# The corner blocks of a triangular inverse: a second path through DRAM replaced by products with the identity

## The chip, the cores and the metric

The kernel runs on one core of a Trainium2 chip. The metric is device time in microseconds (us) of one execution, as the median of several runs. The engines are TensorE (PE; its weight loads are PEld), VectorE (DVE), ScalarE (ACT), GpSimd (POOL) and SyncE (SP), which issues most transfers.

## The reference

Two layers of a decoder trunk on 256 tokens of width 1024: feed-forward, a mixer of three branches, attention to a memory, feed-forward. The change lies in one branch of the mixer, a recurrence with a state per head (8 heads of width 64):

```python
    def step(state, inp):
        r_t, w_t, k_t, v_t, kk_t, a_t = inp
        sa = jnp.einsum('bhij,bhj->bhi', state, kk_t)
        state = (state * w_t[:, :, None, :]
                 - sa[..., None] * (kk_t * a_t)[:, :, None, :]
                 + v_t[..., None] * k_t[:, :, None, :])
        return state, jnp.einsum('bhij,bhj->bhi', state, r_t)
```

The kernel takes it in chunks of 64 tokens, and a chunk needs the inverse of a unit lower triangular 64x64 matrix for each head.

## The kernel before

The trunk is float32. Large products split each weight into a high part (`whi`, by ACT) and a low part (`wlo`, by DVE, from the raw load and `whi`), and take three float32r products for one. Raw weights land in three buffers (`raw0` to `raw2`), the parts in eight each. A raw load on SP therefore waits until DVE has made the last `wlo` from that buffer.

The order on every engine is not written by hand. `Program` records all operations, builds their dependences and orders them with a list scheduler that has costs for each operation. It takes a transfer to last

```python
    DMA_START, DMA_END, DMA_RATE = 1.1, 0.95, 360e3
```

us around its bytes, and records the program several times over, keeping the order that it thinks shortest. So a small edit can move operations anywhere. Each engine then works its list strictly in that order: what stands behind a waiting instruction waits as well.

The tokens are taken in two halves, t = 0 and 1. For each, in each of the two layers, these steps run beside the large products of the mixer; the four solves are called A (layer 0, t=0), B (layer 0, t=1), C (layer 1, t=0) and D (layer 1, t=1).

- `rwkv_front` makes the 64x64 matrices and writes their diagonal 32x32 blocks to DRAM (`sl`), to be read back with one block in each partition (`XL`).
- `rwkv_solve` inverts the 32x32 blocks by 31 elimination steps on DVE. The result `XX` holds, in a partition for each block and group of columns, the columns of the inverse. ACT transposes the free axes of it into `TM` (the "transposing copy", 128x256), SP writes `TM` to DRAM (`sx`, four writes) and reads it back (four reads) into `XT`, where the transposed inverses stand as diagonal blocks. Besides, SP writes `XX` itself to DRAM (`si`, one write) and reads two quarters of it back into `X1` (two reads): the same diagonal blocks, not transposed.
- `rwkv_back` reorders `X1` into `XN` (two ACT copies, 32x256), then fills the off-diagonal corner of the inverse: the products of `LN` and `XT` (16 of 32x32, into banks `b_ya`), two copies by ACT into `HH`, the products of `XN` and `HH` (16 more), and a negated copy into `XT`. The full products with `XT` follow.

The banks of PSUM have four names with two each: `g` for the large products, `ya`, `yb` and `s` for the rest. All operations are issued from one line (L415), so the profile names them by engine and tile: `heap` is the heap that holds XX, TM, XT, X1, XN and HH alike, and `heapr` that of the float32r tiles.

Of the kernel before, what the change touches and what calls it, by code (L numbers as in the profile page):

```python
# [12 lines left out]
F32 = mybir.dt.float32  # L13
# [463 lines left out]
class Trunk:  # L477
# [730 lines left out]
    def rwkv_solve(self, l, t):  # L1208

        nc, h = self.nc, self.h  # L1210
        rt = self.rt[t]
        XL, XX, TM = rt["XL"], rt["XX"], h.alloc(256)
        XT = rt["XT"] = h.alloc(1024)
        nc.gpsimd.memset(XT.ap, 0.0)
        _, sx, si = self.scr[l][t]
        eng = getattr(nc, self.SOLVE)
        xlv = XL.v("p (i j) -> p i j", j=32)
        xx, tm = XX.v("p (i c) -> p i c", c=8), TM.v("p (i c) -> p i c", c=8)
        for j in range(31):
            n, m = 31 - j, j // 4 + 1  # L1220
            self.tt(tm[:, 0:n, 0:m], xlv[:, j + 1:32, j:j + 1].to_broadcast([128, n, m]),
                    xx[:, j:j + 1, 0:m].to_broadcast([128, n, m]), MULT, eng)
            self.tt(xx[:, j + 1:32, 0:m], xx[:, j + 1:32, 0:m], tm[:, 0:n, 0:m], SUB, eng)
        nc.sync.dma_start(si, XX.ap)
        X1 = rt["X1"] = h.alloc(256)
        for q in (0, 2):
            nc.sync.dma_start(X1[32 * q:32 * q + 32, :].rearrange("p (b c) -> p b c", c=8),
                              si.rearrange("(q b) (i c) -> q i b c", q=4, c=8)[q])
        nc.scalar.copy(TM.v("p (c i) -> p c i", c=8), XX.v("p (i c) -> p c i", c=8))
        sxw = sx.rearrange("(b a) (c x i) -> x b (a c) i", a=4, c=2, x=4)  # L1230
        for x in range(4):
            nc.sync.dma_start(sxw[x], TM.v("p (c i) -> p c i", c=8)[x:128:4])
        xt = XT.v("p (h n) -> p h n", h=8)
        sxv = sx.rearrange("(q h a) (c i) -> q (a c) h i", q=4, h=8, c=8)
        for q in range(4):
            nc.sync.dma_start(xt[32 * q:32 * q + 32, :, 32 * q:32 * q + 32], sxv[q])
        h.free(XL, XX, TM)
# [18 lines left out]
    def rwkv_back(self, l, t):  # L1256

        self.rwkv_values(t)
        nc, h = self.nc, self.h
        rt = self.rt[t]  # L1260
        XT, X1, LN, ln, PA, BA, pa, ba, MM, mmv, VS = (
            rt[k] for k in ("XT", "X1", "LN", "ln", "PA", "BA", "pa", "ba", "MM", "mmv", "VS"))
        vs = VS.v("p (c h n) -> p c h n", c=2, h=8)
        xt = XT.v("p (h n) -> p h n", h=8)
        HH = h.alloc(256)
        XN = h.alloc(256)
        for b in (0, 64):
            nc.scalar.copy(XN.v("p (h c x) -> p h c x", h=8, x=4)[b:b + 32], X1.v("p (h x c) -> p h c x", h=8, x=4)[b:b + 32])
        x1, hh = XN.v("p (h n) -> p h n", h=8), HH.v("p (h n) -> p h n", h=8)
        pc = [self.bank("ya", (8, 32)) for _ in range(2)]  # L1270
        for i in range(8):
            for b in (0, 64):
                self.mm(pc[b // 64][b:b + 32, i, :], ln[b + 32:b + 64, i, 0:32], xt[b + 32:b + 64, i, b + 32:b + 64])
        for b in (0, 64):
            nc.scalar.copy(hh[b:b + 32], pc[b // 64][b:b + 32])
        pc = [self.bank("ya", (8, 32)) for _ in range(2)]
        for i in range(8):
            for b in (0, 64):
                self.mm(pc[b // 64][b:b + 32, i, :], x1[b:b + 32, i, :], hh[b:b + 32, i, :])
        for b in (0, 64):  # L1280
            nc.scalar.mul(xt[b:b + 32, :, b + 32:b + 64], pc[b // 64][b:b + 32], -1.0)
        h.free(X1, XN, HH, LN)
        QQ = h.alloc(1024)
        qq = QQ.v("p (h n) -> p h n", h=8)
        for q in range(2):
            ps = self.bank("ya", (4, 128))
            for j in range(4):
                self.mm(ps[:, j, :], xt[:, 4 * q + j, :], pa[:, 4 * q + j, :])
            nc.scalar.copy(qq[:, 4 * q:4 * q + 4, :], ps)
        h.free(XT, PA)  # L1290
        for q in range(2):
            pc = [self.bank("ya", (4, 128)) for _ in range(2)]
            for j in range(4):
                for c in range(2):
                    i = 4 * q + j
                    self.mm(pc[c][:, j, :], qq[64 * c:64 * c + 64, i, :], ba[64 * c:64 * c + 64, i, :])
            for c in range(2):
                m = mmv[:, c, 4 * q:4 * q + 4, :]
                self.tt(m, m, pc[c], SUB)
        h.free(QQ, BA)  # L1300
        rt["Y"] = h.alloc(512)
        if t == 0:
            self.rt[1]["VS"] = h.alloc(1024)
        f4 = self.f64.v("p (h c) -> p h c", h=8)
        for c in range(2):
            ps = self.bank("ya", (8, 64))
            cg = 2 * t + c
            for i in range(8):
                self.mm(ps[:, i, :], mmv[:, c, i, :], vs[:, c, i, :])
            if cg < 3:  # L1310
                nv = self.rt[(cg + 1) // 2]["VS"].v("p (c h n) -> p c h n", c=2, h=8)[0:64, (cg + 1) % 2]
                self.tt(nv, ps[0:64], f4[0:64, :, cg:cg + 1].to_broadcast([64, 8, 64]), MULT)
            nc.scalar.copy(rt["Y"].v("p (h n) -> p h n", h=8)[64 * c:64 * c + 64], ps[64:128])
        h.free(MM, VS)
        if t == 1:
            self.sm.free(self.f64)
# [505 lines left out]
    def run(self):  # L1822
        nc, w = self.nc, self.w
        self.ident = self.tile("ident", [128, 128], F32)
        make_identity(nc, self.ident)
        self.mhalf = self.tile("mhalf", [128, 1], F32)
        nc.gpsimd.memset(self.mhalf, -0.5)
        self.scr = [[(self.tile(f"sl{l}{t}", [32, 32, 32], F32, self.dr), *(self.tile(f"{x}{l}{t}", [128, 256], F32, self.dr) for x in ("sx", "si")))
                     for t in range(2)] for l in range(DEPTH)]

        def into(l, i):

            st = {}

            def nxt(t):
                if t is None:
                    st["gb"] = self.gain(w["norm_g"][l, 2 * i])
                    return
                if t == 0:
                    st["xp"] = self.xpair()  # L1840
                    st["rs"] = [self.sm.alloc(2) for _ in range(2)] if i in (0, 3) else [None, None]
                self.prenorm(self.x[:, t, :], st["gb"], t, st["xp"][2], st["xp"][3], st["rs"][t])
                if t == 1:
                    self.h.free(st["gb"])
            return nxt, st

        def store(t):
            if t is not None:
                for c in self.halves:
                    nc.sync.dma_start(self.out[0, t * 128:t * 128 + 128, c], self.x[:, t, c])  # L1850

        def late():
            self.constants()
            self.rope_tables()

        self.fine = True
        def load(t):
            for c in self.halves:
                nc.scalar.dma_start(self.x[:, t, c], w["x"][0, t * 128:t * 128 + 128, c])

        load(0)
        gb, pair, rs = self.first_gain(w["norm_g"][0, 0]), self.xpair(), [self.sm.alloc(2) for _ in range(2)]
        load(1)
        for t in range(2):
            self.first_norm(self.x[:, t, :], gb, t, pair[2], pair[3], rs[t])
        self.sm.free(gb)
        st = dict(xp=pair, rs=rs)
        for l in range(DEPTH):
            ng = w["norm_g"][l]
            n1, s1 = into(l, 1)  # L1870
            self.ffn(l, 0, st, ng[1], n1, late if l == 0 else None)
            n2, s2 = into(l, 2)
            self.mixer(l, s1, ng[3], n2)
            n3, s3 = into(l, 3)
            self.cross(l, s2, ng[5], n3)
            if l < DEPTH - 1:
                nxt, st = into(l + 1, 0)
            else:
                nxt = store
            self.ffn(l, 1, s3, ng[7], nxt)  # L1880
# [34 lines left out]
```

## Time and profile before

| | us |
|---|---|
| median of 3 runs | 1629.42 |
| lowest and highest | 1627.55, 1633.07 |
| the profiled execution, own time | 1633.05 |
| its span, first to last instruction | 1631.3 |

The mean granted TensorE clock over the span is 0.989. A line of the timeline gives the start, the length, the engine and operation, the tiles written and read, the count, and in brackets the idle time just before on that engine with what ended it. "SPq" is SP's queue of transfers; its length is the time to issue, not to land. The counts x32 in the rows of 32x32 products are for 16 products, since each float32 product is recorded as two.

### The profile page before, as it was taken

To read this page: it belongs to the slowest core of one execution; us is meant where nothing else is said; L and a number is where in the kernel's file an instruction comes from. 1 tells how busy PE (TensorE), PEld (TensorE's weight loads), DVE (VectorE), ACT (ScalarE), POOL (GpSimd) and SP (SyncE) were. 2 spreads that over 40 slices of the span, in tenths; PEclk is the share of its full clock that TensorE was granted. 3 is DMA by queue.
4 is the path that set the end of the run, shared out by engine and by line. 5 is a ranking of instruction groups with operands and counts; after the bars stand their busy time and mean duration, and the time that the engine had idled before them with its cause. 6 is when DMAs were issued, how large, how long until landed. Compare 5 with 4: busy or idle time off the path is not lost.

```text
span 1631.3 us, 23864 instructions
## 1 busy us (share of the span) xinstructions
PE 1587.8 (97%) x8644; PEld 1327.7 (81%) x8644; DVE 1085.2 (67%) x2109; ACT 962.8 (59%) x1891; POOL 116.3 (7%) x209
## 2 busy tenths in 40 slices
PE   8999999899999999999999999999999999999998
PEld 6888789787778987888878887997787789878886
DVE  6555668769777567555575566587797775675555
ACT  5555576768555556555565455868675465565553
POOL 7000011000110001000010001100001010010000
PEclk9999999999999999999999999999999999999999
DMA  8555544422755545656546555434236565354652
GB/s 281 177 195 192 161 128 149 147 94 93 227 178 195 188 139 172 207 179 201 186 158 201 187 189 159 141 126 142 94 120 219 173 199 181 121 182 162 210 180 94
DMA packets 209467, 274.40 MB, mean 168 GB/s; under 512 B 32284, under 2 KB 161282, under 8 KB 209348
## 3 DMA queue, kind: packets, MB, share of 16 engines
q1 hardware_dynamic: 208756, 271.81, 50.9%
q8 instruction: 68, 1.11, 0.3%
q10 hardware_dynamic: 592, 1.05, 0.2%
q14 instruction: 51, 0.42, 0.1%
HBM read 270.08 MB, written 2.75 MB: 167 GB/s over the span
## 4 chain that ended last, share of the span: by engine, by line
PE 79%; DVE 11%; ACT 4%; DMA 2%; issue 2%; SPq 1%; POOL 0%; DVEq 0%; ACTq 0%
PE b_g L415 42%; PE b_ya L415 15%; PE b_s L415 12%; PE b_yb L415 10%; DVE heap L415 6%; DVE wlo L415 3%; ACT heap L415 2%; ACT whi L415 1%; DMA heap<-sx 1%; DMA heap<-sl 1%; DMA raw<-in_w_ffn_in_dram 1%; DVE zq L415 1%; SPq L415 1%; DVE x L415 1%; DVE heapr L415 0%
## 5 line engine op out<-in xcount | busy, mean ns | idle before, releaser
L415 DVE TENSOR_TENSOR wlo<-raw,whi 128x512 fp32r<-128x512 f32 (+1 forms) x964 | 648.2, 688 | 385.3 <-ACT whi L415 378.8
L415 ACT CAST whi<-raw 128x512 fp32r<-128x512 f32 (+1 forms) x964 | 583.6, 620 | 456.2 <-PE b_g L415 224.3
L415 PE MATMUL b_g<-whi,heapr 128*128 128x512 f32 (+2 forms) x1904 | 653.9, 404 | 4.5 <-ACT heapr L415 2.9
L415 PEld LDWEIGHTS b_g<-whi,heapr 128*128 128x128 f32 x1904 | 356.8, 190 | 85.4 <-ACT heapr L415 6.7
L415 PE MATMUL b_g<-wlo,heapr 128*128 128x512 f32 (+2 forms) x952 | 368.9, 402 | 2.2 <-DVE wlo L415 2.2
L415 PEld LDWEIGHTS b_g<-wlo,heapr 128*128 128x128 f32 x952 | 180.6, 190 | 38.7 <-DVE wlo L415 3.4
L415 PE MATMUL b_g<-heapr,whi 128*128 128x256 f32 x1104 | 199.0, 288 | 1.7 <-DVE heap L415 1.0
L415 PE MATMUL b_ya<-whi,heapr 128*128 128x512 f32 x480 | 177.2, 394 | 0.0
L415 PE MATMUL b_yb<-whi,heapr 128*128 128x512 f32 x480 | 176.3, 393 | 0.0
L415 PE MATMUL b_s<-whi,heapr 128*128 128x512 f32 x448 | 175.4, 399 | 0.5 <-DVE heap L415 0.5
L415 PEld LDWEIGHTS b_g<-heapr,whi 128*128 128x128 f32 x1104 | 163.1, 191 | 5.9 <-DVE heap L415 2.1
L415 PE MATMUL b_g<-heapr,wlo 128*128 128x256 f32 x552 | 132.1, 289 | 0.0
L415 DVE TENSOR_TENSOR heap<-heap 128x256 f32<-128x256 f32 (+24 forms) x376 | 112.8, 315 | 12.6 <-ACT heap L415 4.9
L415 POOL TENSOR_SCALAR small<-small 128x1 f32<-128x1 f32 (+2 forms) x52 | 28.2, 543 | 1275.1 <-ACT heap L415 1112.4
L415 PEld LDWEIGHTS b_yb<-whi,heapr 128*128 128x128 f32 x480 | 89.8, 188 | 18.6 <-DVE heapr L415 0.2
L415 PEld LDWEIGHTS b_ya<-whi,heapr 128*128 128x128 f32 x480 | 89.3, 188 | 18.7 <-ACT heap L415 0.2
L415 ACT CAST heapr<-b_s 128x256 fp32r<-128x256 f32 (+2 forms) x144 | 63.0, 439 | 64.2 <-PE b_s L415 56.9
L415 PEld LDWEIGHTS b_s<-whi,heapr 128*128 128x128 f32 x448 | 83.8, 188 | 19.5 <-DVE heap L415 1.6
L415 PE MATMUL b_s<-ident,heap 128*128 128x128 f32 x433 | 91.7, 276 | 5.5 <-DVE heap L415 4.7
L415 PEld LDWEIGHTS b_g<-heapr,wlo 128*128 128x128 f32 x552 | 93.8, 191 | 1.6 <-issue 0.5
L415 DVE TENSOR_TENSOR heapr<-b_s,heapr 128x256 fp32r<-128x256 f32 (+2 forms) x144 | 72.6, 505 | 32.3 <-ACT heapr L415 31.9
L415 PE MATMUL b_ya<-wlo,heapr 128*128 128x512 f32 x240 | 93.0, 392 | 0.0
(167 smaller groups left out, 1562.8 us busy)
## 6 DMA issues: line engine op xcount, KB each, us to landing
raw<-in_w_ffn_in_dram SPq DMA_DIRECT2D x172, 512.0 KB
raw<-in_w_in_dram SPq DMA_DIRECT2D x50, 1024.0 KB
raw<-in_w_ffn_out_dram SPq DMA_DIRECT2D x44, 1024.0 KB
raw<-in_mem_wkv_dram SPq DMA_DIRECT2D x16, 1024.0 KB
raw<-in_w_branch_dram SPq DMA_DIRECT2D x12, 1024.0 KB
raw<-in_w_out_dram SPq DMA_DIRECT2D x8, 1024.0 KB
raw<-in_mem_wq_dram SPq DMA_DIRECT2D x8, 1024.0 KB
raw<-in_mem_wo_dram SPq DMA_DIRECT2D x8, 1024.0 KB
```

The lines of the kernel that those rows point to most:

```text
L415: getattr(eng.real, method)(*a, **k)
```

## The change

`rwkv_solve` no longer writes and reads `si`, and `rwkv_back` no longer reorders `X1`. Instead, 16 products of 32x32 with the identity turn the diagonal blocks of `XT` back, into two banks `s`, and DVE copies those into `X1`. The DRAM tensors `si` go.

```diff
-        _, sx, si = self.scr[l][t]
+        _, sx = self.scr[l][t]
...
-        nc.sync.dma_start(si, XX.ap)
-        X1 = rt["X1"] = h.alloc(256)
-        for q in (0, 2):
-            nc.sync.dma_start(X1[32 * q:32 * q + 32, :].rearrange("p (b c) -> p b c", c=8),
-                              si.rearrange("(q b) (i c) -> q i b c", q=4, c=8)[q])
...
-        HH = h.alloc(256)
-        XN = h.alloc(256)
-        for b in (0, 64):
-            nc.scalar.copy(XN.v("p (h c x) -> p h c x", h=8, x=4)[b:b + 32], X1.v("p (h x c) -> p h c x", h=8, x=4)[b:b + 32])
-        x1, hh = XN.v("p (h n) -> p h n", h=8), HH.v("p (h n) -> p h n", h=8)
-        pc = [self.bank("ya", (8, 32)) for _ in range(2)]
+        HH, X1 = h.alloc(256), h.alloc(256)
+        x1, hh = X1.v("p (h n) -> p h n", h=8), HH.v("p (h n) -> p h n", h=8)
+        pc, px = ([self.bank(x, (8, 32)) for _ in range(2)] for x in ("ya", "s"))
         for i in range(8):
             for b in (0, 64):
                 self.mm(pc[b // 64][b:b + 32, i, :], ln[b + 32:b + 64, i, 0:32], xt[b + 32:b + 64, i, b + 32:b + 64])
+        for i in range(8):
+            for b in (0, 64):
+                self.mm(px[b // 64][b:b + 32, i, :], xt[b:b + 32, i, b:b + 32], self.ident[b:b + 32, b:b + 32])
         for b in (0, 64):
             nc.scalar.copy(hh[b:b + 32], pc[b // 64][b:b + 32])
+        for b in (0, 64):
+            nc.vector.tensor_copy(x1[b:b + 32], px[b // 64][b:b + 32])
...
-        h.free(X1, XN, HH, LN)
+        h.free(X1, HH, LN)
```

The scheduler makes a new order of the whole program from it. Three places of it follow; a number behind a tile's name tells buffers apart, and the waits are those on other engines or transfers.

SP at B, from the writes of `sx` to its reads, before:

```order
L415 DMA sx01_100<-heap_71 256x1x32 [waits DMAHW7_49]
L415 DMA raw0_75<-in_w_in_dram 128x4x512 [waits DMAHW0_49,DVE_49]
L415 DMA heap_71<-si01_101 32x32x8 [waits DMAHW3_49,DMAHW1_49]
L415 DMA heap_71<-si01_101 32x32x8 [waits DMAHW2_49]
L415 DMA heap_71<-sx01_100 32x8x32 [waits DMAHW6_49,DMAHW5_49,DMAHW7_49,DMAHW4_49,Pool_49]
L415 DMA heap_71<-sx01_100 32x8x32 x3
```

and after:

```order
L415 DMA sx01_99<-heap_71 256x1x32 [waits DMAHW3_49]
L415 DMA raw1_76<-in_w_in_dram 128x4x512 [waits DMAHW4_49,DVE_49]
L415 DMA heap_71<-sx01_99 32x8x32 [waits DMAHW2_49,DMAHW3_49,DMAHW1_49,DMAHW5_49,DMAHW0_49,Pool_49]
L415 DMA heap_71<-sx01_99 32x8x32 [waits DMAHW6_49]
L415 DMA heap_71<-sx01_99 32x8x32 [waits DMAHW7_49]
```

The reads of `si` are gone. One raw load still stands between, now of the next buffer: before, its DVE wait was for the last `wlo` of `raw0` (`wlo1`, the next to be used when ACT makes its transposing copy), after, for the last of `raw1` (`wlo5`, four casts on). At D it is the same: before `wlo3`, after `wlo7`. At A no raw load is left between the writes and the reads of `sx`; at C one is left.

ACT at B, from the transposing copy on, before:

```order
L415 COPY heap_71<-heap_71 128x256 [waits DMAHW5_49,DVE_49]
L415 CAST whi2_80<-raw1_76 128x512 [waits DMAHW5_49,PE_49,Activation_49]
L415 ACTIVATE heap_71<-b_g1_64 128x512 [waits PE_49]
L415 CAST whi3_81<-raw1_76 128x512 [waits PE_49,Activation_49]
L415 CAST whi4_82<-raw1_76 128x512 [waits PE_49,Activation_49]
L415 ACTIVATE heap_71<-b_g0_63 128x512 [waits PE_49]
L415 CAST whi5_83<-raw1_76 128x512 [waits Activation_49]
L415 CAST whi6_84<-raw2_77 128x512 [waits DMAHW1_49,PE_49,Activation_49]
L415 COPY heap_71<-heap_71 32x256 [waits DMAHW3_49,DMAHW1_49,Activation_49]
L415 COPY heap_71<-heap_71 32x256 [waits DMAHW2_49]
L415 CAST whi7_85<-raw2_77 128x512 [waits PE_49]
L415 COPY heap_71<-b_ya0_65 32x256 [waits PE_49]
```

and after:

```order
L415 COPY heap_71<-heap_71 128x256 [waits DVE_49]
L415 CAST whi3_81<-raw1_76 128x512 [waits PE_49,Activation_49]
L415 CAST whi4_82<-raw1_76 128x512 [waits PE_49,Activation_49]
L415 ACTIVATE heap_71<-b_g0_63 128x512 [waits PE_49]
L415 CAST whi5_83<-raw1_76 128x512 [waits Activation_49]
L415 CAST whi6_84<-raw2_77 128x512 [waits DMAHW5_49,PE_49,Activation_49]
L415 CAST whi7_85<-raw2_77 128x512 [waits PE_49,Activation_49]
L415 CAST whi0_78<-raw2_77 128x512 [waits PE_49,Activation_49]
L415 CAST whi1_79<-raw2_77 128x512 [waits PE_49,Activation_49]
L415 COPY heap_71<-b_ya0_65 32x256 [waits PE_49,Activation_49]
```

The two 32x256 copies of `X1`, which waited for `si`, are gone, and two more casts stand ahead of the copy of the first small products. The transposing copy itself comes one cast later.

TensorE at B, around the first small products, before:

```order
L415 MATMUL b_g0_63<-whi0_78,heapr_72 128x512
L415 MATMUL b_g0_63<-wlo0_86,heapr_72 128x512
L415 MATMUL b_ya0_65<-heap_71 32x32 [waits DMAHW3_49,Pool_49]
L415 MATMUL b_ya1_66<-heap_71 32x32 [waits DMAHW4_49]
L415 MATMUL b_ya0_65<-heap_71 32x32
```

and after:

```order
L415 MATMUL b_g1_64<-whi4_82,heapr_72 128x512
L415 MATMUL b_g1_64<-whi5_83,heapr_72 128x512 [waits Activation_49]
L415 MATMUL b_g1_64<-wlo5_91,heapr_72 128x512
L415 MATMUL b_s1_70<-ident_94,heap_71 32x32 [waits DMAHW5_49,Pool_49]
L415 MATMUL b_ya0_65<-heap_71 32x32 [waits DMAHW6_49]
L415 MATMUL b_ya1_66<-heap_71 32x32 [waits DMAHW7_49]
L415 MATMUL b_s0_69<-ident_94,heap_71 32x32 [waits DMAHW0_49]
```

Fifteen more products of the same stream (the rest of `whi0`, `whi1` to `whi4` and two of `whi5`) stand ahead of the small ones; at D it is sixteen. The new products mix with the old.

Counted over the order: casts `whi` between ACT's transposing copies of A and B are 53 before and 44 after, of C and D 46 and 44; DVE rows between the ends of the solves A and B are 212 and 179; table loads on ACT are 38 and 46 in the program. The only products that are added are the 64 of 32x32 with the identity.

More of the change, by code (lines that the diff above doesn't have):

```diff
@@ L1260, in rwkv_back @@
         rt = self.rt[t]
-        XT, X1, LN, ln, PA, BA, pa, ba, MM, mmv, VS = (
-            rt[k] for k in ("XT", "X1", "LN", "ln", "PA", "BA", "pa", "ba", "MM", "mmv", "VS"))
+        XT, LN, ln, PA, BA, pa, ba, MM, mmv, VS = (
+            rt[k] for k in ("XT", "LN", "ln", "PA", "BA", "pa", "ba", "MM", "mmv", "VS"))
         vs = VS.v("p (c h n) -> p c h n", c=2, h=8)
         xt = XT.v("p (h n) -> p h n", h=8)
-        HH = h.alloc(256)
-        XN = h.alloc(256)
-        for b in (0, 64):
-            nc.scalar.copy(XN.v("p (h c x) -> p h c x", h=8, x=4)[b:b + 32], X1.v("p (h x c) -> p h c x", h=8, x=4)[b:b + 32])
-        x1, hh = XN.v("p (h n) -> p h n", h=8), HH.v("p (h n) -> p h n", h=8)
-        pc = [self.bank("ya", (8, 32)) for _ in range(2)]
+        HH, X1 = h.alloc(256), h.alloc(256)
+        x1, hh = X1.v("p (h n) -> p h n", h=8), HH.v("p (h n) -> p h n", h=8)
+        pc, px = ([self.bank(x, (8, 32)) for _ in range(2)] for x in ("ya", "s"))
         for i in range(8):
@@ L1827, in run @@
         nc.gpsimd.memset(self.mhalf, -0.5)
-        self.scr = [[(self.tile(f"sl{l}{t}", [32, 32, 32], F32, self.dr), *(self.tile(f"{x}{l}{t}", [128, 256], F32, self.dr) for x in ("sx", "si")))
+        self.scr = [[(self.tile(f"sl{l}{t}", [32, 32, 32], F32, self.dr), self.tile(f"sx{l}{t}", [128, 256], F32, self.dr))
                      for t in range(2)] for l in range(DEPTH)]
```

## The prediction

> **What bounds the kernel now.** The page first, since it says which engine sets the time.
>
> ```profile
> span 1631.3 us, 23864 instructions
> PE 1587.8 (97%) x8644; PEld 1327.7 (81%) x8644; DVE 1085.2 (67%) x2109; ACT 962.8 (59%) x1891; POOL 116.3 (7%) x209
> ```
>
> TensorE is busy for 97% of the span, so only two things can shorten the program: TensorE's 43.5 us of idle time, and the places where its work runs slowly. Next I asked who waits for the transfers that the change touches (waits: us in total, times, longest).
>
> ```profile
> ACT heap L415 <- DMA heap<-si: 7.6, 4, 2.5
> ...
> PE b_ya L415 <- DMA heap<-sx: 5.6, 4, 2.9
> ```
>
> All four solves show in both rows. I call them A and B (layer 0, token halves 0 and 1), C and D (layer 1). TensorE's timeline around them gives the idle time in brackets:
>
> ```profile
> 317.70 0.64 PE L415 MATMUL b_yb<-ident,heap 128*96 128x128 f32 x4 [1.29 <-ACT heap L415]
> 319.95 1.16 PE L415 MATMUL b_yb<-heap 96*128 96x128 f32 x8 [0.58 <-ACT heap L415]
> 321.45 0.78 PE L415 MATMUL b_ya<-heap 32*32 32x32 f32 x32 [0.34 <-DMA heap<-sx]
> ...
> 438.46 0.62 PE L415 MATMUL b_g<-whi,heapr 128*128 128x512 f32 x2
> 438.92 0.39 PE L415 MATMUL b_g<-wlo,heapr 128*128 128x512 f32 x1
> 442.22 1.14 PE L415 MATMUL b_ya<-heap 32*32 32x32 f32 x32 [2.92 <-DMA heap<-sx]
> ...
> 1134.91 0.66 PE L415 MATMUL b_s<-heap 128*64 128x128 f32 x8 [1.68 <-ACT heap L415]
> 1136.70 0.85 PE L415 MATMUL b_ya<-heap 32*32 32x32 f32 x32 [0.41 <-DMA heap<-sx]
> ...
> 1246.42 1.30 PE L415 MATMUL b_ya<-heap 32*32 32x32 f32 x32 [1.94 <-DMA heap<-sx]
> ```
>
> Idle: A 2.21, B 2.92, C 2.09, D 1.94, together 9.2 us. Then the granted clock of the stretches around B, C and D, of B's idle time, and of A's stretch (columns: length, busy time of PE, PEld, DVE, ACT, POOL, granted clock, DMA share, GB/s):
>
> ```profile
> 438.30:448.30 10.00, 7.08 (x82) 5.54 (x81) 3.36 (x5) 4.09 (x9) 0.00 (x0) 0.66 0.77 221
> 1133.20:1144.80 11.60, 9.48 (x100) 7.56 (x100) 3.59 (x7) 6.88 (x18) 0.00 (x0) 0.71 0.27 83
> 1244.30:1254.20 9.90, 7.85 (x85) 6.50 (x85) 2.68 (x5) 4.89 (x10) 0.00 (x0) 0.66 0.69 183
> ...
> 440.00:442.00 2.00, 0.00 (x0) 0.00 (x0) 0.46 (x1) 1.04 (x2) 0.00 (x0) 0.84 0.49 63
> ...
> 316.40:326.40 10.00, 7.66 (x108) 5.55 (x108) 5.21 (x10) 8.42 (x26) 0.52 (x1) 1.00 0.74 225
> ```
>
> After B, C and D the clock falls: (1-0.66)x10.0, (1-0.71)x11.6 and (1-0.66)x9.9 are each 3.4 us, 10.2 in all, of which (1-0.84)x2.0 = 0.3 falls on B's idle time: 9.9 us lost. After A, whose idle time is split in three, it stays at 1.00. So the four places cost 9.2 + 9.9 = 19 us.
>
> The Trainium skill ("TensorE: Matmul & The Clock Gate", section "Why this matters for your kernels") says that gaps of up to about 3 us between bursts keep the clock up. By that rule the 9.9 us would not be there to win, and the gain below would be 6.6 us smaller. The rows differ: gaps of 2.92, 1.94, and 1.68 with 0.41 are each followed by half clock, so I go by the rows.
>
> **Why TensorE waits there.** SP's queue at B and D, and ACT's copies:
>
> ```profile
> 434.86 0.55 SPq L415 DMA_DIRECT2D raw<-in_w_in_dram  x1
> 435.51 1.05 SPq L415 DMA_DIRECT2D heap<-si  x2
> 436.74 4.54 SPq L415 DMA_DIRECT2D heap<-sx  x4
> ...
> 1239.83 0.55 SPq L415 DMA_DIRECT2D raw<-in_w_in_dram  x1
> ...
> 310.46 0.66 ACT L415 COPY heap<-heap 128x256 f32<-128x256 f32 x1
> ...
> 431.57 0.69 ACT L415 COPY heap<-heap 128x256 f32<-128x256 f32 x1
> ...
> 440.93 1.30 ACT L415 COPY heap<-heap 32x256 f32<-32x256 f32 x2 [2.53 <-DMA heap<-si]
> ...
> 1125.40 0.74 ACT L415 COPY heap<-heap 128x256 f32<-128x256 f32 x1
> ...
> 1236.54 0.69 ACT L415 COPY heap<-heap 128x256 f32<-128x256 f32 x1
> ```
>
> The reads of sx stand behind those of si on the queue. ACT stands still until si lands, with casts of weights behind it.
>
> **The change, part by part.** 1. *The si path goes.* Its two reads hold SP for 1.05 us ahead of sx; the pieces that they move (32 bytes each) also stand ahead of sx in the transfer queue, which no row prices alone. So sx lands earlier, counted from the weight load before it, by 1.05 us or more; the lower bound is 0 (that load alone decides), the upper the whole step from one issue to the next, 436.74-435.51 = 1.2. I take 1.1. The write of si holds SP at another time and hides.
>
> 2. *ACT loses* eight 32x256 copies and the wait before them (groups: count, busy us, mean ns, idle before):
>
> ```profile
> L415 ACT COPY heap<-heap 32x256 f32<-32x256 f32 x8 | 5.2, 644 | 7.7 <-DMA heap<-si 7.6
> ...
> L415 PE MATMUL b_ya<-heap 32*32 32x32 f32 x256 | 8.0, 219 | 5.7 <-DMA heap<-sx 5.6
> ...
> L415 ACT ACT_TABLE_LOAD x38 | 48.8, 1283 | 10.8 <-DMA x<-in_x_dram 4.3 <-DVE small L415 4.0 <-PE b_g L415 1.9
> ...
> L415 DVE COPY heap<-heap 128x256 f32<-128x256 f32 x2 | 0.6, 277 | 0.0
> ```
>
> 5.2 + 7.6 us leave ACT. At A and C this is what TensorE waited for (the 1.29, 0.58 and 1.68 <-ACT above).
>
> 3. *TensorE gains* 64 products of 32x32, in four groups of 16. Eight such groups take 8.0 us now, 1.0 each, and A's only 0.78 at full clock: between 3.1 and 4.3 us for four. They need the same sx as the products beside them, so nothing hides them. I take 3.3.
>
> 4. *DVE gains* eight 32x256 copies out of PSUM. No row shows one; ACT's copy of that size takes 644 ns, DVE's of twice the partitions and more 277, so 2.2 to 5.2 us in all. TensorE has a few weight products between the groups, so I charge 0, at most 8x0.64 = 5.2 if nothing covers them. Behind them on DVE stand splits of weights, whose buffers are eight deep; the second group of products (x1 by hh) now waits for DVE's copies as well as ACT's, which run side by side.
>
> 5. *The order moves, which decides most.* At B fifteen more 128x512 products stand ahead of the first small one, at D sixteen. Two such start between 438.46 and 438.92, so one in 0.23 us: TensorE, which stopped at 442.22-2.92 = 439.3 and 1246.42-1.94 = 1244.5, gets there at 439.3+3.5 = 442.8 and 1244.5+3.7 = 1248.2. But the weight load ahead of sx on SP now waits for a later split on DVE, the last of its buffer:
>
> ```profile
> 436.76 0.69 DVE L415 TENSOR_TENSOR wlo<-raw,whi 128x512 fp32r<-128x512 f32 x1 [1.02 <-ACT whi L415]
> ...
> 1241.94 0.69 DVE L415 TENSOR_TENSOR wlo<-raw,whi 128x512 fp32r<-128x512 f32 x1 [1.12 <-ACT whi L415]
> ```
>
> These end at 437.45 and 1242.63; with the load's 0.55 the queue is free at 438.0 and 1243.2. Before, 442.22-435.41 = 6.8 and 1246.42-1240.38 = 6.0 us passed from the load's end to the products, si included; less 1.1 they come at 443.7 and 1248.1. So the idle time falls to 0.9 at B and to nothing at D, where I leave 0.1. At C twenty-six such products (6.0) and six groups of float32 products and transposes, at 0.6 as those at 317.70 and 1134.91, stand behind ACT's transposing copy, 9.6 us. Before, 1136.70-1125.40 = 11.3 us passed there; less 1.1, and less the wait of ACT, that leaves 0.5. At A the load no longer stands between write and read of sx; I take 0.5 too. The rest is 2.0 of 9.2: **-7.2 us**, bounds 0 and -9.2.
>
> 6. *The clock.* With under 1 us of idle time I expect the clock to hold at three of four, as after A. The small products, two groups in a row, are themselves light work (1.6 us), so one fall (3.3) is left: **-6.6 us**; bounds -9.9 (none) and +3.3 (all four).
>
> 7. *Table loads on ACT* go from 38 to 46 in the order: 8x1.283 = 10.3 us, in the mixer, less than the 12.8 that part 2 frees there. TensorE pays between 0 and 10.3; near the lower end, since ACT is 59% busy: **+2**.
>
> Sum: -7.2 -6.6 +3.3 +2 = -8.5 us. The profiled execution took 1633.05 us, its span 1631.3; less 8.5 that is 1624.5. It was 3.6 above the median of the runs, 1629.42, so the median goes to 1621.
>
> **The rivals.** *The clock still falls after every solve* (0.20). For it: the fall after C followed idle pieces of only 1.68 and 0.41, and light products grow from 1.6 to 2.4 us a solve. Against: A. Price: clock +3.3 instead of -6.6, small products at half clock 4.3: -7.2+3.3+4.3+2 = +2.4, so 1632, no change. The Trainium skill's same page (section "Part 4: PE-mode transpose") says that transposes do not count as TensorE work for the clock; by it this rival would be likelier, if a product with the identity counts as one. No run here shows it.
>
> *All four places heal* (0.20): no fall of the clock, table loads hidden, products at 0.78: -7.2-9.9+3.1 = -14.0, so 1615.5. For it: D's arithmetic closes to nothing.
>
> *The chain from one solve to the next can't be shortened* (0.15), the slower case. The order puts 44 weight casts between ACT's transposing copies of A and B, where 53 stood, and 44 for 46 between C and D. The rows of part 1 give 431.57-310.46 = 121.1 us for 53 and 1236.54-1125.40 = 111.1 for 46, 2.3 to 2.4 us a cast. If the chain (back, front, sl through DRAM, 31 steps on DVE) needs 111 us, 44 casts cover 103.4 and TensorE idles 7.7 us twice: -8.5+15.4 = +6.9, so 1636.5. It decides from a chain of about 107.5 us on. Against: DVE rows between the solves fall from 212 to 179 at A-B, so less stands in the chain's way.
>
> *That the change does not do what it says*: the order has no si row left, so I give it nothing.
>
> **How the numbers follow.** The forecast has 0.45, with 1617 to 1626 as its own range (table loads from 0 to 5 us, and the idle time at two places off by 1 us either way). 0.3% is 4.9 us, about what a measurement can tell here, so faster means below 1624.5: 0.37 of the 0.45 and the 0.20 that heals, 0.57. Slower, over 1634.3: 0.15 and a little of the clock's case, 0.18. The rest, 0.25, is the same. The range takes in the healed case and most of the slower one: 1613 to 1636.
>
> **What would show it.** In the trace after: no si; SP's sx reads right behind the weight load; idle time before the small products under 1 us at each solve; clock 1.00 around three of them; 64 products b_s<-ident,heap of 32x32 in some 3 us; 46 table loads with TensorE busy beside them. I am wrong if the clock falls at three or four solves, if TensorE idles over 3 us between A and B or C and D on sl or DVE, or if gaps appear in the mixer behind table loads.

## The result, and the profile after

The changed kernel takes 1638.62 us (median of 6 runs, 1634.62 to 1639.73) against 1629.84 for the kernel before beside it: a ratio of 1.0051 with a 95% interval of 1.0038 to 1.0063, so 8.8 us or half a per cent slower. I had forecast 1621. The profiled execution is the longest of the six; its span is 6.6 us longer than that of before.

```profile
span 1637.9 us, 24094 instructions
PE 1595.8 (97%) x8772; PEld 1333.9 (81%) x8772; DVE 1087.1 (66%) x2117; ACT 969.5 (59%) x1891; POOL 115.0 (7%) x209
```

TensorE is busy 8.0 us longer, and its idle time has hardly shrunk (43.5 to 42.1 us). Nor has the clock's loss: summed over the whole program in stretches of 2 us, it is 17.5 us before and 17.1 after. At the solves themselves, though, most of what was promised is there. TensorE's timeline at A (343), B (451), C (1146 and 1152) and D (1255), with the idle time in brackets:

```profile
343.19 1.02 PE L415 MATMUL b_s<-ident,heap 32*32 32x32 f32 x32 [0.36 <-DMA heap<-sx]
...
451.67 0.22 PE L415 MATMUL b_s<-ident,heap 32*32 32x32 f32 x2 [0.23 <-DMA heap<-sx]
...
1146.95 0.66 PE L415 MATMUL b_s<-heap 128*64 128x128 f32 x8 [0.83 <-ACT heap L415]
...
1152.35 0.68 PE L415 MATMUL b_s<-ident,heap 32*32 32x32 f32 x27 [1.12 <-DMA heap<-sx]
...
1255.89 0.22 PE L415 MATMUL b_s<-ident,heap 32*32 32x32 f32 x2 [1.10 <-DMA heap<-sx]
```

That is 0.36 + 0.23 + 1.95 + 1.10 = 3.64 us of idle time, where 9.16 stood. The granted clock (third number from the right) around the program's start, the four solves and one more place that comes up below:

```profile
30.00:46.00 16.00, 12.88 (x48) 10.10 (x47) 10.58 (x32) 5.37 (x14) 5.07 (x15) 0.79 0.67 216
341.00:351.00 10.00, 9.56 (x128) 8.06 (x127) 3.69 (x7) 4.45 (x11) 0.00 (x0) 0.83 0.45 133
446.00:456.00 10.00, 9.74 (x129) 7.04 (x129) 8.30 (x14) 4.58 (x9) 0.00 (x0) 1.00 0.94 271
1144.00:1156.00 12.00, 10.04 (x142) 7.58 (x142) 5.70 (x10) 10.57 (x20) 0.00 (x0) 1.00 0.42 111
1252.00:1264.00 12.00, 10.83 (x130) 8.91 (x128) 6.00 (x11) 3.30 (x7) 0.00 (x0) 0.75 0.77 258
376.00:388.00 12.00, 9.62 (x44) 7.70 (x43) 10.19 (x37) 10.89 (x18) 0.00 (x0) 0.86 0.65 216
```

B and C hold the full clock now; A loses 0.17 x 10 = 1.7 us and D 0.25 x 12 = 3.0 and, in the 2 us behind its row, another 0.4 (clock 0.82), together 5.1 where 9.9 stood. So in these two executions the solves gained 5.5 + 4.8 us. The groups show what was paid (before's row of the 64x128 products was 24.8 us at 286 ns):

```profile
L415 ACT ACT_TABLE_LOAD x46 | 59.0, 1283 | 9.2 <-DMA x<-in_x_dram 4.3 <-DVE small L415 2.5 <-PE b_g L415 1.4
...
L415 PE MATMUL b_ya<-heap 64*128 64x128 f32 x256 | 28.4, 288 | 0.2
...
L415 PE MATMUL b_s<-ident,heap 32*32 32x32 f32 x128 | 3.6, 192 | 2.9 <-DMA heap<-sx 2.8
L415 DVE COPY heap<-b_s 32x256 f32<-32x256 f32 x8 | 3.3, 417 | 3.1 <-PE b_s L415 3.0
```

**The program's start**, 300 us ahead of any solve, lost 4 us. It is the order on VectorE. In the changed kernel the cast of the positions, which waits for their transfer, and seven operations that follow from it stand ahead of the low part (`heapr<-b_s,heapr`) for which TensorE waits (VectorE's rows, then TensorE's):

```profile
33.67 0.17 DVE L415 CAST small<-posi 128x2 f32<-128x2 int32 x1 [2.48 <-DMA posi<-in_positions_dram]
33.95 1.67 DVE L415 TENSOR_SCALAR small<-small 128x16 f32<-128x16 f32 x5
35.66 0.42 DVE L415 SCALAR_TENSOR_TENSOR small<-small 128x32 f32<-128x32 f32 x2
35.99 0.69 DVE L415 TENSOR_TENSOR wlo<-raw,whi 128x512 fp32r<-128x512 f32 x1
36.60 0.42 DVE L415 TENSOR_TENSOR heapr<-b_s,heapr 128x256 fp32r<-128x256 f32 x1
```

```profile
37.07 0.69 PE L415 MATMUL b_s<-ident,heap 128*128 128x128 f32 x2 [3.12 <-DVE heapr L415]
```

In the kernel before, the cast of the positions ends 0.5 us earlier, one such operation stands ahead of the same low part and the rest behind it, and TensorE waits 0.77 us:

```profile
33.42 0.26 DVE L415 TENSOR_SCALAR small<-small 128x16 f32<-128x16 f32 x1
33.57 0.69 DVE L415 TENSOR_TENSOR wlo<-raw,whi 128x512 fp32r<-128x512 f32 x1
34.17 0.42 DVE L415 TENSOR_TENSOR heapr<-b_s,heapr 128x256 fp32r<-128x256 f32 x1
34.50 1.47 DVE L415 TENSOR_SCALAR small<-small 128x16 f32<-128x16 f32 x3
```

```profile
34.64 0.44 PE L415 MATMUL b_s<-ident,heap 128*128 128x128 f32 x2 [0.77 <-DVE heapr L415]
```

The changed kernel has 3.12 us of idle time here, and then 0.21 x 16 = 3.4 us of clock. None of these instructions is touched by the diff: the planner made another order. ScalarE's sine of the rotary tables waits for the same chain, but TensorE doesn't wait for it, since it comes 0.6 us behind the start of TensorE's row:

```profile
37.67 0.23 ACT L415 ACTIVATE sin<-small 128x32 f32<-128x32 f32 x1 [3.12 <-DVE small L415]
```

**The attention's outputs** are the other thing that moved. The view of the tile b_s on TensorE between 305 and 390 us, the kernel before and then the changed one (first and last start of the 48 products of attention by values, 128x64):

```profile
L415 PE MATMUL b_s<-heap x48: 272/273/323, 313.5 to 372.0; 128*64 128x128 f32 x48
```

```profile
L415 PE MATMUL b_s<-heap x48: 272/273/323, 321.3 to 339.8; 128*64 128x128 f32 x48
```

Before, 16 of them came ahead of A's first small product (321.45) and 32 behind it. Now all 48 come ahead, and A's products start at 343.19, 21.7 us later. In layer 1 it is the same. They have to: the new products write the two s banks, the attention's outputs write the same two banks, and they are recorded earlier.

### The profile page after: what moved, and what is told of

It reads as the page before. It is cut to its first block, busy times and chain, and to the rows that moved or that the text cites. A ratio compares the mean times of both kernels' runs of the same rounds, so it can differ in the third digit from the quotient of the medians.

```text
span 1637.9 us, 24094 instructions
## 1 busy us (share of the span) xinstructions
PE 1595.8 (97%) x8772; PEld 1333.9 (81%) x8772; DVE 1087.1 (66%) x2117; ACT 969.5 (59%) x1891; POOL 115.0 (7%) x209
## 5 line engine op out<-in xcount | busy, mean ns | idle before, releaser
L415 PE MATMUL b_g<-heapr,whi 128*128 128x256 f32 x1104 | 202.5, 291 | 0.2
L415 DVE TENSOR_TENSOR heap<-heap 128x256 f32<-128x256 f32 (+26 forms) x376 | 111.4, 315 | 6.2 <-DMA heap<-sl 1.2
L415 PE MATMUL b_s<-ident,heap 128*128 128x128 f32 (+1 forms) x561 | 95.0, 257 | 10.7 <-DVE heap L415 4.7
```

What stands on the lines that cost most here:

```text
L415: getattr(eng.real, method)(*a, **k)
```

## The experiments

VectorE makes 964 low halves of weight splits, in the same sequence in every kernel here, so the end of number n, counted from 0, is a milestone. The table gives its time in the profile of before and how many us later each kernel's profile has it: after the start (n = 32), at the end of the first feed-forward block (136), behind the mixer of layer 0 (280), ahead of the mixer of layer 1 (608), behind it (752), and near the end (960). These are single executions (that of before was 3.6 us above its median, so a drift can read that much too low); the medians, with the ratio to before and its 95% interval, stand on the right.

| kernel | 32 | 136 | 280 | 608 | 752 | 960 | median us | ratio |
|---|---|---|---|---|---|---|---|---|
| before (time) | 51.9 | 201.6 | 506.8 | 992.4 | 1296.8 | 1611.2 | | |
| changed | 4.2 | 4.1 | 5.4 | 5.1 | 6.9 | 7.7 | 1638.6 | 1.0051 (1.0038-1.0063) |
| e1 old start | -0.1 | -0.1 | -1.2 | -1.5 | 0.4 | 1.0 | 1633.7 | 1.0022 (1.0011-1.0034) |
| e2 edit in old order | -0.5 | -0.5 | -2.4 | -2.7 | -7.1 | -6.9 | 1626.4 | 0.9981 (0.9968-0.9994) |
| e3 strip's banks | -1.8 | -1.9 | -8.1 | -8.2 | -10.7 | -10.4 | 1623.0 | 0.9956 (0.9942-0.9970) |
| e4 before, planned anew | -0.9 | -1.1 | -0.1 | 0.3 | 5.9 | 6.4 | 1631.0 | 1.0008 (0.9994-1.0022) |
| e5 old order, s banks | -0.1 | -0.3 | 31.1 | 30.9 | 58.7 | 58.7 | 1688.3 | 1.0352 (1.0330-1.0373) |
| e6 old order, no si | -1.0 | -1.1 | -4.4 | -4.7 | -11.0 | -11.0 | 1622.2 | 0.9950 (0.9931-0.9968) |
| e7 changed, second plan | -1.2 | -1.3 | -0.7 | 0.1 | 2.8 | 3.1 | 1635.5 | 1.0033 (1.0018-1.0048) |
| e8 strip's banks, second plan | 0.3 | 0.3 | -5.2 | -4.9 | -9.0 | -8.6 | 1623.9 | 0.9961 (0.9945-0.9976) |
| e9 strip's banks, changed order | 2.5 | 2.5 | 6.3 | 6.1 | 12.6 | 13.2 | 1643.2 | 1.0088 (1.0076-1.0100) |
| e10 before, changed start | 1.0 | 0.9 | 3.9 | 3.8 | 1.7 | 1.7 | 1631.3 | 1.0017 (1.0007-1.0027) |
| e11 changed, third plan | 1.3 | 1.3 | 1.6 | 1.7 | 5.1 | 5.6 | 1638.3 | 1.0051 (1.0035-1.0067) |
| e12 strip's banks, third plan | 2.5 | 2.7 | 6.3 | 7.0 | 4.9 | 4.8 | 1632.9 | 1.0010 (0.9995-1.0024) |

Nothing outside the start and the two mixers drifts by more than about 1 us in any of them.

**e1: the old start.** Both kernels are planned in one file, and an instruction that the plan of before starts in its first 60 us keeps that place:

```
-        best.issue(best.schedule)
+        one, two = plan(True), plan(False)
+        one.issue(one.start(two))
```

> The changed kernel with one thing put back: what its plan issues in the first 60 us stands in the order of the kernel before (28 rows of VectorE, 9 of ScalarE, 48 of GpSimd and 8 of SyncE move, no row of TensorE). Theory A, half of the loss has nothing to do with the solves but is the order of the first feed-forward block, where ScalarE's sine stands ahead of a cast and waits 3.12 us for the positions: the 4.2 us lost by 60 us come back and stay, about 1634.4 us. Rival, the later stages are bound by something else and would have waited anyway: 1637 to 1639 us, and the drift of 4.2 us reappears before 480 us.

1633.7 us, 4.9 less than the changed kernel, and the drift at the start is gone: theory A. 3.7 us over before are left by the medians; in the profile it is the second mixer that loses (1.9). The run puts rows of four engines back, so it shows what the order of the start costs, and not that the sine does it: by the rows above, VectorE's order holds TensorE.

**e10: the mirror**, the kernel before with the changed kernel's start.

> The kernel before, without the edit, but with the order that the changed kernel has in its first 60 us (the mirror of the run that put the old start into the changed kernel). Theory A, the start's loss belongs to the order and not to the edit: 4 to 5 us slower than before, 1633 to 1635 us, with the wait of 3 us at 37 us and a fall of the clock there. Rival, the start only loses together with the edit: 1629 to 1631 us.

1631.3 us, 2.3 slower than before, half of what I expected and just above the rival's range. TensorE's row at the place:

```profile
36.45 0.44 PE L457 MATMUL b_s<-ident,heap 128*128 128x128 f32 x2 [1.72 <-DVE heapr L457]
```

The wait is there, but 1.72 us long, and no fall of the clock follows. So this order costs by itself (the interval lies above 1), but less without the fall: 1.0 us at the first milestone here, 2.5 in e9, whose start is the same, 4.2 in the changed kernel.

**e2: the edit alone.** The plan, the buffers and the place of each instruction are those of before; only the edit's own instructions differ. The small products write the partitions that the strip's products leave free in their own two banks:

```
+    base = min(progs, key=lambda p: p.span)
+    best = k.record(None, base)
...
+        px = pc[::-1]
```

> The edit alone: every instruction that both kernels have stands where the kernel before has it, on every engine and in the same buffers; the path through si and the 8 ScalarE copies are taken out, the 64 small products stand right behind the 64 products of the strip, with their 8 VectorE copies, and they write the free partitions of the strip's own two banks (so that no other user of a bank has to move). Theory A, the edit itself is good or harmless and the re-made order lost: sx lands about 1.1 us earlier at each solve, the small products cost 0.5 to 0.9 us there, so 0 to 3 us less than before, 1627 to 1630 us. Rival, the edit itself costs what the mixers lost (1.3 and 1.8 us) or more: 1632 to 1635 us.

1626.4 us, 3.6 less than before, just faster than expected: with the strip's banks and in the old order, the edit pays. What it pays in is seen beside e6.

**e6: the removal without the addition.**

```
-                nc.scalar.copy(XN.v("p (h c x) -> p h c x", h=8, x=4)[b:b + 32], X1.v(...)[b:b + 32])
+                nc.scalar.copy(XN.v("p (h n) -> p h n", h=8)[b:b + 32], self.ident[b:b + 32, b:b + 32].unsqueeze(1)...)
```

> The order of the kernel before with the path through si taken out and nothing put in its place: the two ScalarE copies read blocks of the identity, so the corner blocks are left out of the result. Theory A, the gain is the earlier landing of sx (1.1 us at each solve, and fewer falls of the clock), and the small products with their copies cost about 2 us of TensorE and a wait of 0.7 to 1.6 us at each solve: 1620 to 1624 us, 3 to 6 us below the run with them. Rival, the products and copies lie in time that was idle anyway: 1625 to 1628 us, the same as with them.

1622.2 us, 4.1 below e2: theory A. (This kernel leaves the corner blocks out of the result.) At B the SyncE and the TensorE row:

```profile
431.11 0.55 SPq L455 DMA_DIRECT2D raw<-in_w_in_dram  x1
```

```profile
437.31 1.15 PE L455 MATMUL b_ya<-heap 32*32 32x32 f32 x32 [1.79 <-DMA heap<-sx]
```

From the load's end (431.66) to the products are 5.65 us, where 6.8 stood: 1.16 us earlier (at D 0.83). Against the 4.1 us between e2 and e6 stand the products (2.8 us of TensorE in e2) and, in e2, waits for VectorE's copies ahead of the second small products, at B, C and D:

```profile
442.11 0.69 PE L455 MATMUL b_ya<-heap 32*32 32x32 f32 x32 [0.70 <-DVE heap L455]
...
1134.42 0.69 PE L455 MATMUL b_ya<-heap 32*32 32x32 f32 x32 [1.65 <-DVE heap L455]
...
1243.63 0.69 PE L455 MATMUL b_ya<-heap 32*32 32x32 f32 x32 [0.70 <-DVE heap L455]
```

With 3.05 us of waits that is 5.9, more than 4.1: at B and C the clock lost 3.4 us each in e6's profile and 1.7 each in e2's, so the split is rough.

**e5: the same with the s banks.** The one line of e2 that names the banks is put back:

```
-        px = pc[::-1]
+        px = [self.bank("s", (8, 32)) for _ in range(2)]
```

> The edit in the order of the kernel before, as in the run of that kind with the strip's banks, but the small products write the two s banks, as the change has it. Nothing is planned anew: each instruction stands where the kernel before has it, or right behind the last one it must now wait for; by that 418 rows of TensorE shift, some by 165 places, since the attention's outputs use the same banks ahead of the small products and the next front's transposes behind. Theory B, the s banks are what hurts: 3 to 12 us slower than with the strip's banks, 1630 to 1639 us. Rival, only the new plan hurt and the banks don't matter: within 1.5 us of 1626.4.

1688.3 us, 62 more than e2, far more than expected. TensorE's timeline shows why (pieces around A, then the wait that ends the first mixer's trouble):

```profile
319.64 0.78 PE L455 MATMUL b_ya<-heap 32*32 32x32 f32 x32 [0.97 <-DMA heap<-sx]
...
335.38 0.69 PE L455 MATMUL b_s<-ident,heap 32*32 32x32 f32 x16 [0.86 <-ACT heap L455]
336.65 0.80 PE L455 MATMUL b_ya<-heap 32*32 32x32 f32 x16 [0.58 <-DVE heap L455]
...
408.42 1.22 PE L455 MATMUL b_yb<-trig,heap 128*128 128x128 f32 x4 [9.53 <-DVE heap L455]
```

The strip's products come at 319.64, but the new products come at 335.38, behind the attention's outputs, and all of the second solve's front with them: its first step on SyncE, the write of sl, moves from 357.0 (e2) to 391.7, VectorE waits 8.15 us for it and TensorE 9.53 for VectorE. So the banks are a link in the chain from one solve to the next. A planner can't keep before's order with them.

**e3: the changed kernel with the strip's banks**, planned anew:

```
-        pc, px = ([self.bank(x, (8, 32)) for _ in range(2)] for x in ("ya", "s"))
+        pc = [self.bank("ya", (8, 32)) for _ in range(2)]
+        px = pc[::-1]
```

> The changed kernel with the small products in the free partitions of the strip's own two banks instead of the two s banks, planned anew. Theory B, the s banks tie the chain at the solve to the attention outputs ahead and to the next front's transposes behind, and that is what the mixers lose: the mixers come out at or below the kernel before, 1622 to 1630 us with a start like before's, 4 us more with a start like the changed kernel's. Rival, the banks don't matter and any new plan of this edit loses in the mixers: 1633 to 1640 us.

1623.0 us: 7.0 faster than before and 15.6 faster than the changed kernel. It is the version that beats both. The view of b_s, the groups and a row of A:

```profile
L415 PE MATMUL b_s<-heap x48: 272/273/323, 312.9 to 365.1; 128*64 128x128 f32 x48
```

```profile
L415 ACT ACT_TABLE_LOAD x38 | 48.8, 1283 | 8.8 <-DMA x<-in_x_dram 4.3 <-DVE small L415 2.5 <-PE b_g L415 1.4
L415 PE MATMUL b_ya<-heap 64*128 64x128 f32 x256 | 25.5, 286 | 0.1
...
L415 PE MATMUL b_ya<-ident,heap 32*32 32x32 f32 x128 | 2.8, 192 | 0.0
```

```profile
315.26 0.67 PE L415 MATMUL b_ya<-heap 32*32 32x32 f32 x27 [1.23 <-DMA heap<-sx]
```

Eight attention outputs stand ahead of A's products and 40 behind; A comes 27.9 us earlier than in the changed kernel, the 64x128 products are back near 24.8, and the table loads at 38.

**e9: the strip's banks in the changed kernel's order.**

> The small products in the strip's banks, but in the order of the changed kernel, which was planned for the s banks (no row of the other engines moves by more than 2 places, 120 of TensorE by up to 24). Theory B, the s banks cost nothing while the program runs, only by the order that they force on the plan (all attention outputs ahead of the first solve's products): the time stays where the changed kernel's is, 1636 to 1640 us. Rival, the banks themselves are slow (products and copies wait for each other's bank at run time): 5 us or more come back, below 1633.

1643.2 us: nothing comes back. It is 4.6 us slower than the changed kernel and above the range that I gave; that the order was not made for these banks may be why, but no run shows it. So no cost of the s banks while the program runs is seen; they cost through the order that they force.

**e4, e7, e8, e11, e12: other plans.** To tell the banks from the luck of a plan, one constant of the planner is changed:

```
-    ALPHA, PENALTY = 0.1, 8
+    ALPHA, PENALTY = 0.099, 8
```

(e11: 0.1 and 6; e12: 0.08 and 6.) The kernel before:

> The kernel before with no edit, but one constant of its planner at 0.099 instead of 0.1, so that the same work gets another order. Theory A, a new order alone is worth several us at the start and in the mixers either way: the time moves by 2 to 8 us from 1629.8, and the drift against before jumps at the start or in the mixers. Rival, orders of this planner are alike: within 1.5 us of before, and drift under 1 us in every stage.

1631.0 us, not told apart from before: the rival on the time. Its profiled execution, at 1638.7 us, was 7.7 above its own median, so its drift of 6 us in the second mixer isn't evidence for either.

The changed kernel:

> The changed kernel with the planner's constant at 0.099. Theory B, whatever the order, the s banks cost the mixers: 1632 to 1641 us, and 44 or more table loads. Rival, the changed kernel's own order was bad luck: below 1630 us.

> The changed kernel (small products in the s banks) with another constant of the planner, the penalty for switching ScalarE's table, at 6 instead of 8; of the plans seen for it this is the one that the planner itself counts shortest (1585.6, against 1587.5 for the changed kernel and 1580.6 for the kernel before). Theory B, the s banks hold the first solve's products behind all attention outputs in any plan: not faster than before, 1629 to 1637 us. Rival, with a lucky plan the change pays as it stands: below 1626 us.

1635.5 and 1638.3 us: no plan of the three makes it pay. e7 loses nothing at its start and has only 38 table loads, so these two are not what makes the mixers slow. Its 48 attention outputs still lie together (310.1 to 328.6), and its 64x128 products take 27.9 us, e11's 28.4. In e7 the first of A's strip products start among those outputs (316.53) and only the new products come behind the last (329.83): in all three plans the s banks hold back the new products, in two of them the strip's as well.

The strip's banks:

> The kernel with the small products in the strip's banks, with the planner's constant at 0.099. Theory B, 1621 to 1629 us, below the kernel before by up to 8 us, and 4 us or more below the changed kernel with the same constant. Rival, the 1623.0 us of the first was a lucky order: 1630 to 1636 us, no better than the changed kernel with the same constant.

> The small products in the strip's banks, planned with the constants 0.08 and 6, the shortest that the planner counts for it (1579.7, against 1581.1 for the first of this kind). Theory B, any plan with these banks is faster than before: 1618 to 1626 us. Rival, plans scatter by more than the banks are worth: above 1629 us.

1623.9 us bears theory B out; 1632.9 doesn't. e12 is no faster than before, so "any plan" was too much. Its rows show two places ahead of any solve, each followed by a fall of the clock:

```profile
36.38 0.33 PE L415 MATMUL b_s<-ident,heap 128*128 128x128 f32 x1 [1.93 <-DVE heapr L415]
...
289.20 0.71 PE L415 MATMUL b_g<-heapr,whi 128*128 128x256 f32 x2 [2.50 <-DVE heap L415]
```

Three plans with the s banks lie at 1635.5 to 1638.6, three with the strip's at 1623.0 to 1632.9: the banks are worth 11 us on the mean, though the nearest two lie 2.6 us apart, and a plan scatters by up to 10. By the planner's own count, quoted in the expectations, e12 was the shortest of its three, so it can't rank plans this close.

## Why the prediction was wrong, point by point

**Right: the price of the wait.** Part 1's 1.1 us for the si path measured 1.16 and 0.83 (e6). Part 2's copies are gone. Part 3's 3.3 us for the products are 3.6 by the changed kernel's group, 2.8 with the strip's banks.

**Right in sign, too large: parts 5 and 6 at the solves.** Idle time fell by 5.5 us (I said 7.2), the clock's loss by 4.8 (I said 6.6, with three of four places healed; it is two). "Under 1 us at each solve" held at A and B, not at C and D. The clock's part is in part luck. I took it that A keeps the full clock since its idle time is split; e10, whose order on TensorE is that of before from end to end and whose idle time there is split the same way (1.35 and 0.59 us), loses 0.42 x 12 = 5.0 us behind it:

```profile
318.00:330.00 12.00, 11.39 (x107) 8.70 (x108) 5.14 (x10) 7.62 (x23) 0.52 (x1) 0.58 0.51 161
```

**Right: part 4.** VectorE's copies take 3.3 us, inside the bounds. I charged 0 for TensorE, and in the changed kernel it has no wait for them ahead of the second small products; in the old order it has 0.70 + 1.65 + 0.70 = 3.05 us (e2).

**Not separated: part 7.** I charged the eight more table loads 2 us and placed them beside other work. What they cost TensorE no run tells. One load stands in a wait of TensorE that the kernel before doesn't have (ScalarE's and TensorE's rows of the changed kernel):

```profile
378.84 1.14 ACT L415 CAST whi<-raw 128x512 fp32r<-128x512 f32 x2
379.88 0.37 ACT L415 COPY heap<-b_yb 128x256 f32<-128x256 f32 x1
380.15 0.62 ACT L415 CAST whi<-raw 128x512 fp32r<-128x512 f32 x1
380.79 1.28 ACT L415 ACT_TABLE_LOAD   x1
382.08 1.09 ACT L415 ACTIVATE heap<-b_g 128x512 f32<-128x512 f32 x2
```

```profile
382.73 0.50 PE L415 MATMUL b_g<-whi,heapr 128*128 128x512 f32 x1 [2.38 <-ACT heap L415]
```

With the clock after it, 0.14 x 12 = 1.7, that is 4.1 us at one place. I had named such gaps as what would make me wrong. But the load is only 1.28 of the 2.38 us, and loads stand as close in the kernel before (five from 367 to 383 us, as here from 370 to 385), where TensorE waits 0.58 us at most: it is where the order puts them on ScalarE. e1 and e9, which have the same order here, have the same wait (2.38 and 2.37 us), e9 without the fall of the clock.

**The step that failed: part 5, "the order moves, which decides most".** I priced the order at the four solves alone and took the rest of the program as unmoved. What moved elsewhere, against before: +4.2 us at the start, +4.1 at the wait for ScalarE at 382.73, +3.6 in the 64x128 products, fewer of which start in pairs in the new order (last section), and +1.9 in TensorE's waits for VectorE between the solves (A to B 2.2 before and 1.5 after, C to D 1.7 and 4.3). With the solves (-5.5 - 4.8 + 3.6 = -6.7) this makes +7.1 where the span grew by 6.6; the sum is rough. So the gains that I forecast at the solves came for the most part, and the same order lost more elsewhere than they brought.

**What I didn't see was in the diff.** The line that takes the banks for the new products names "s", and I read it as free space. The attention's outputs use these banks ahead and the next front's transposes behind. The order I had in hand said it: "44 weight casts between ACT's transposing copies of A and B, where 53 stood". I asked whether the chain between A and B could be that short. It can: 105.4 us pass between the two copies, and VectorE doesn't wait long for sl (1.2 us in all). A had moved back by 21.7 us and B by 9.4, so that the distance shrank from the wrong end.

**The rivals.** The slower one (put at 1636.5, though 1629.4 + 6.9 is 1636.3) came within 2.3 us of the time, but not by its mechanism: TensorE has no wait of 7.7 us between the solves. Between C and D it does wait 4.3 us for VectorE, over the 3 us that I had named as a sign, in pieces of 1.6 us and less. The clock's rival (1632) is half right: falls remain at two solves, and others came at 37 and 384 us. The healed case would have been nearest to e3, in which none of the four solves has a fall behind it, 1623.0 us.

**Shown and open.** Shown: in before's order and with the strip's banks the edit pays (e2), the s banks destroy that order (e5) and the strip's banks allow a good one (e3, e8) without helping at run time (e9); the start's loss belongs to the order (e1, and in part e10). Open: what share of the bank's price comes from the attention's outputs ahead and what from the front's transposes behind, which no run separates; what the table loads cost; how much of each difference in the clock is chance; and why e12's plan loses 3.6 us in the first mixer.

## What to carry to other kernels

A buffer that the diff calls free must be looked up: who uses it ahead of the new work and who behind, in the order of recording, since sharing it is a dependency like any other. Where a planner orders the whole program, price an edit once in the old order, held fixed, and once in the new; the first tells what the edit is worth, the difference what the plan made of it. And where plans of the same work scatter by as much as the gain sought, one plan is one draw: time two or three before keeping or dropping the edit.

## What the runs showed of the hardware

The clock doesn't follow the length of the gap alone. In the changed kernel 1.10 us of idle time at D, with the small products behind it, was followed by 0.75 over 12 us, 0.36 at A by 0.83 over 10, while 0.83 and 1.12 at C left it at 1.00; e10's 1.72 us at its start left it whole, too. And with the same order on TensorE, pieces of 1.35 and 0.59 us at A are followed by 0.58 over 12 us in e10, pieces of 1.29, 0.58 and 0.34 by 1.00 over 10 in the kernel before. The Trainium skill ("TensorE: Matmul & The Clock Gate", section "Why this matters for your kernels") lets gaps of up to about 3 us pass; by D's and A's rows it does not hold here. The same page's free-running window of about 3.4 us (section "What's actually happening") fits better: the losses of 1.7 and 3.4 us in the rows above are half of one such window and of two. By it a gap would count by what else lies in its window; no row here shows where the windows lie.

How much products of 64x128 overlap depends on how they stand. Two rows of TensorE's timeline, the kernel before and the changed one:

```profile
338.39 1.16 PE L415 MATMUL b_ya<-heap 64*128 64x128 f32 x16
```

```profile
365.29 1.16 PE L415 MATMUL b_ya<-heap 64*128 64x128 f32 x8
```

Sixteen take 1.16 us in the one place and eight as long in the other, though a single one takes the same 286 and 288 ns by the groups: 24.8 us for all 256 before, 28.4 in the changed kernel. In the trace the sixteen start in pairs, 7 ns apart, and the eight one by one, about 112 ns apart; of the changed kernel's runs of sixteen, those in pairs take 1.16 us and those one by one up to 2.38.
